# Block two of a two-block transformer kernel: the order of the projection groups, the gates, and who does four small pieces of work

## The chip, the cores and the metric

The kernel runs on one core of a Trainium2 chip. The metric is the device time of one execution in microseconds (us); of several runs of one kernel the median counts. The profiled execution is a run of its own, and the trace divides its time among the engines: TensorE (PE, with its weight loads as PEld), VectorE (DVE), ScalarE (ACT), GpSimd (POOL) and SyncE (SP), which issues the DMAs.

## The reference, cut to what matters

The program is two transformer blocks of two layers each over 256 positions of width 1024, all in float32. The change touches only block two. One of its layers:

```python
h = rmsnorm(x, g_mix)
(qa, ka, va, qb, kb, vb, fl, qc, kc, vc, qi, ki, wi, gl) = split(h @ w_in)
br_a = stick_breaking_attention(qa, ka, va)          # w = exp(log_beta + later sums of log(1 - beta))
br_b = forgetting_attention(qb, kb, vb, cumsum(log_sigmoid(fl + b_forget)))
br_c = indexed_sparse_attention(rope(qc), rope(kc), vc, rope(qi), rope(ki), wi, top_k=64)
gates = sigmoid(gl)                                  # three gates of width 1024
y = gates[0] * (br_a @ w_branch[0]) + gates[1] * (br_b @ w_branch[1]) + gates[2] * (br_c @ w_branch[2])
x = x + y @ w_out
x = x + square(relu(rmsnorm(x, g_mlp) @ w_up)) @ w_down
```

`br_a` has 8 heads of 64, `br_b` 8 heads, `br_c` 8 query heads over 2 key heads; queries and keys are 256 positions, handled as two blocks `tb` of 128.

## The kernel before, in words

**Products.** Each float32 operand is held as two parts, a rounded high part and the rest, and each product is three matmuls (`mm3`, lines 290 to 292). A weight unit is 256 rows by 512 columns; ScalarE rounds it (line 265) and VectorE subtracts to get the rest (line 267; GpSimd does it for a few units of the first group). Units are loaded six ahead and split three ahead, in the order of the list `units`.

**Groups.** A projection of 512 columns is a group of four units. `proj` keeps the activations stationary and gives rows of positions: per unit 12 matmuls of 512 columns. `projT` keeps the weights stationary and gives the transposed result: per unit 24 matmuls of 256 columns. In block two the value groups VA and VB use `proj`, whose evacuation is one ScalarE copy per `tb`; the query and key groups QA, KA, QB, KB use `projT`, whose evacuation is a multiply on VectorE and a split on ScalarE and VectorE. The order is ORDER2: KCQI, QC, the small group TAIL (key of the index, forget logits, index weights), QB, KB, VB, QA, KA, VA, then for each of three merges (branch c, b, a) gate half 0, product half 0, gate half 1, product half 1, then the output projection `w_out` and the MLP.

**Tasks and turns.** The attention work is written as Python generators (tasks) in a queue. `tick()` takes the next two tasks and runs each to its next `yield`, which is a turn. `proj` calls `tick` once per unit and `tb` (8 times a group), `projT` twice per unit and pair of column blocks (16 times a group). So a turn's place is fixed by where the main loop is. The tasks of a layer are `ki_task` and `lf_task` (index key; log of the forget gates, its running sum by TensorE at line 1630), `dsa_task` (index scores, then eight rounds of `max` and `match_replace` per `tb` for the top 64, lines 1666 to 1668, then attention over four pairs of heads), `fox_task` (attention of branch b over four pairs), and `sb_task` (stick-breaking). `join` runs a task to its end, and stands ahead of the first product of its branch. Below that, the Tile framework orders each engine's instructions when the program is built: by place in the program, but an instruction whose operands it estimates to be late lets later ones pass. What comes out is one fixed order per engine; on the chip an engine waits at the head of its list.

**`attend`** (lines 1462 to 1489), for one pair of heads and one `tb`: scores by TensorE; bias and row maximum by VectorE (1471); exponentials and row sums by ScalarE (1476); reciprocal and two multiplies by VectorE (1478, 1480); after one `yield` the transposes by TensorE (1485); their copies by VectorE and ScalarE (1489).

**`sb_task`**: six score tiles of 128x512; Abs and Exp by ScalarE; then per tile Ln by ScalarE (1780), an add by VectorE (1781), a mask by VectorE (1788), another by GpSimd (1790), with a `yield` after every second tile; then per tile a rounded copy and the rest, both by GpSimd (1796, 1798); then the sums over positions as matmuls with a triangle, the high part first (1802) and the rest behind it (1803); Exp; the products with the values (1821, 1822).

**`merge_tok`** (line 1402): gates through tanh on ScalarE (1410), products gated by VectorE (1419) and added up by GpSimd or, for the last branch, by VectorE (1427). The last branch's sums are transposed by small tasks that begin with two empty turns (`Yt.put`), and the output projection follows.

Of the kernel before, what the change touches and what calls it, by code (L numbers as in the profile page):

```python
# [11 lines left out]
F32 = mybir.dt.float32  # L12
# [7 lines left out]
P = 128  # L20
# [18 lines left out]

KCQI, QC, QA, KA, VA, QB, KB, VB, GL = range(9)  # L40
TAIL = -1
ORDER2 = [KCQI, QC, TAIL, QB, KB, VB, QA, KA, VA]
MERGE2 = (2, 1, 0)


# [55 lines left out]
def two_block_kernel(ctx: ExitStack, tc: tile.TileContext, A, out):  # L101
# [28 lines left out]
    def t2(shape, dtype=F32):  # L130

        return T(kp, shape, "k2", dtype)
# [39 lines left out]
    def spawn(gen):  # L172
        t = Task(gen)
        tasks.append(t)
        return t
# [10 lines left out]
    def serial(*gens):  # L186
        for g in gens:
            yield from g
# [38 lines left out]
    for l in range(DEPTH):  # L227
        slowly(1 + l)
        for n in ORDER2:
            if n == TAIL:  # L230
                units += [A["w_tail"][l]]
            else:
                units += [A["w_in_2"][l, n, k] for k in range(4)]
        for b in MERGE2:
            for c in range(2):
                units += [A["w_in_2"][l, GL + 2 * b + c, k] for k in range(4)]
                units += [A["w_bo_2"][l, b, c, k] for k in range(2)]
        for c in range(2):
            units += [A["w_out_2"][l, c, k] for k in range(4)]
        for f in range(9):  # L240
            if f == 0:
                slowly(3)
            if f < 8:
                units += [A["w_up"][l, f, k] for k in range(4)]
            if f:
                units += [A["w_down"][l, c, 2 * (f - 1) + k] for k in range(2) for c in range(2)]
# [637 lines left out]
        for l in range(DEPTH):  # L884
            dve.tensor_scalar(nlam[:, l:l + 1], lam[:, l:l + 1], LAM_INIT[l], -1.0, op0=ALU.add, op1=ALU.mult)

    def neg_log1p_exp(o, x, n, pool_):

        e = T(pool_, [P, n], "lp_e")
        a = T(pool_, [P, n], "lp_a")  # L890
        s = T(pool_, [P, n], "lp_s")
        q = T(pool_, [P, n], "lp_q")
        dve.scalar_tensor_tensor(a, x, -1.0, x, op0=ALU.mult, op1=ALU.max)
        act.activation(e, a, AF.Exp, scale=-1.0)
        dve.tensor_scalar(a, e, 2.0, None, op0=ALU.add)
        dve.reciprocal(a, a)
        dve.tensor_tensor(s, e, a, op=ALU.mult)
        dve.tensor_tensor(q, s, s, op=ALU.mult)
        dve.memset(e, 1.0 / 19)
        for k in range(8, -1, -1):  # L900
            dve.tensor_tensor(e, e, q, op=ALU.mult)
            dve.tensor_scalar(e, e, 1.0 / (2 * k + 1), None, op0=ALU.add)
            yield
        dve.tensor_tensor(e, e, s, op=ALU.mult)
        dve.tensor_scalar(a, x, 0.0, None, op0=ALU.min)
        dve.scalar_tensor_tensor(o, e, -2.0, a, op0=ALU.mult, op1=ALU.add)
# [492 lines left out]
                split(*yT.t[k], y.pop(k), scale=0.5)  # L1399
            projT(2, operands, ev_o, n=n, ticks=1)  # L1400

    def merge_tok(bi, acts, waits, oT, operands, y, yT, rms=None):


        for c in range(2):
            gt = {}

            def ev_gate(tb, ps):
                t = gt[tb] = t2([P, 512])
                act.activation(t, ps, AF.Tanh, scale=rms(tb, True) if rms else 0.5)  # L1410
            if c == 0:
                ts = waits + [spawn(serial(after(waits), g)) for g in oT]
            proj(4, acts, ev_gate)
            if c == 0:
                join(ts)

            def ev_o(tb, ps):
                t = gt.pop(tb)
                dve.scalar_tensor_tensor(t, t, 1.0, ps, op0=ALU.add, op1=ALU.mult)
                if bi == 0:  # L1420
                    y[tb, c] = t
                    return
                ys = y[tb, c]
                if bi == 1:
                    pool.tensor_tensor(ys, ys, t, op=ALU.add)
                    return
                dve.tensor_tensor(ys, ys, t, op=ALU.add)
                yT.put(tb, c, y.pop((tb, c)), 2)
            proj(2, {tb: operands(tb) for tb in acts}, ev_o)

    def by_block(br):

# [9 lines left out]
    xb = [xb[0], xb[1]]  # L1442


    SHE, SLE = pool, pool
    tri = cp.tile([P, 2, P], F32R, name="tri")
    dve.tensor_copy(tri[:, 0], C("negge"))
    dve.tensor_copy(tri[:, 1], C("negone"))
# [13 lines left out]
    def attend(tb, pair, scores, bias, v, pT):  # L1462

        S_ = P * (tb + 1)
        ps = sm_bank()[:, :2 * S_].rearrange("p (j s) -> p j s", j=2)
        scores(ps, tb, pair, S_)
        yield
        z = t2([P, 2, 256])[:, :, :S_]
        st = small(8)
        for j in range(2):  # L1470
            dve.tensor_tensor_reduce(z[:, j], ps[:, j], bias(tb, 2 * pair + j), 1.0, -3.0e38,
                                     op0=ALU.add, op1=ALU.max, accum_out=st[:, j:j + 1])
        dve.tensor_scalar(st[:, 2:4], st[:, 0:2], -1.0, None, op0=ALU.mult)
        yield
        for j in range(2):
            act.activation(z[:, j], z[:, j], AF.Exp, bias=st[:, 2 + j:3 + j], accum_out=st[:, 4 + j:5 + j])
        yield
        dve.reciprocal(st[:, 6:8], st[:, 4:6])
        for j in range(2):
            dve.tensor_scalar(z[:, j], z[:, j], st[:, 6 + j:7 + j], None, op0=ALU.mult)  # L1480
        yield
        pt = sm_bank()[:, :2 * S_].rearrange("p (j s) -> p j s", j=2)
        for j in range(2):
            for sb in range(tb + 1):
                pe.transpose(pt[:, j, sb * P:(sb + 1) * P], z[:, j, sb * P:(sb + 1) * P], ident)  # L1485
        yield
        for j in range(2):
            o = pT[j][:, 0:P] if tb == 0 else pT[j][:, P:3 * P]
            (act.copy if j else dve.tensor_copy)(o, pt[:, j])
# [11 lines left out]
    def block2_layer(l, hT, rms):  # L1501
# [114 lines left out]
        def lf_task():  # L1616
            yield from after([t_ki])

            f2 = lambda t: t.rearrange("p a b -> p (a b)")
            yield from neg_log1p_exp(f2(lf), f2(lfx), 16, tp)  # L1620
            lf2 = T(tp, [P, 2, 40], "lf2")
            pool.memset(lf2, 0.0)
            for k in range(2):
                dve.tensor_copy(lf2[:, :, 32 * k:32 * k + 8], lf)

            nlo = cst[:, COFF["negle"][0]:COFF["negle"][0] + 256]
            for _ in range(LFY):
                yield
            ps = sm_bank()[0:40, 0:256]
            pe.matmul(ps, lf2[:, 0], nlo, start=True, stop=False)  # L1630
            pe.matmul(ps[:, P:], lf2[:, 1], nlo[:, :P], start=False, stop=True)
            yield
            par = C("par")
            for k in range(2):
                act.activation(cs[0:40, k], ps, AF.Copy, scale=par[0:40, k:k + 1])
            for k in range(2):
                dve.scalar_tensor_tensor(cs[32:40, k], ps[32:40], par[32:40, k:k + 1], cs[32:40, k].bitcast(F32),
                                         op0=ALU.mult, op1=ALU.subtract)
# [4 lines left out]
        def dsa_task():  # L1643
            yield from after(t_c + [t_ki])
            for tb in range(2):
# [4 lines left out]
                for p_ in range(2):  # L1650
# [6 lines left out]
                    for j in range(2):  # L1657
# [2 lines left out]
                            dve.tensor_scalar(scv, r[:, j], wv[:, 0:1], None, op0=ALU.mult)  # L1660
                        else:
                            dve.scalar_tensor_tensor(scv, r[:, j], wv[:, i:i + 1], scv, op0=ALU.mult, op1=ALU.add)
                    yield
                dve.tensor_tensor(scv[:, tb * P:], scv[:, tb * P:], causal, op=ALU.add)
                m8 = small(8)
                for it in range(8):
# [4 lines left out]
                dve.tensor_scalar(M, scv, -2.0e38, -NEG, op0=ALU.is_lt, op1=ALU.mult)  # L1671
                dve.tensor_scalar(M, M, NEG, None, op0=ALU.add)
                dve.tensor_tensor(M[:, tb * P:], M[:, tb * P:], causal, op=ALU.add)
                yield

            def scores(ps, tb, pair, S_):
                qh, ql = (t[:, pair % 2, tb * P:(tb + 1) * P] for t in qcT[pair // 2])
# [10 lines left out]
        t_dsa = spawn(dsa_task())  # L1688


        qbT = [(t2([P, 2, 256], F32R), t2([P, 2, 256], F32R)) for _ in range(2)]
        kbdB = [(zeros4(), zeros4()) for _ in range(2)]

# [7 lines left out]
                r = slice(64 * j, 64 * j + 64)  # L1701
                split(*(t[r, :, j] for t in kbdB[q]), ps[r])
        projT(4, hT.mov, ev_kb)
        vb = {}

        def ev_vb(tb, ps):
            vb[tb] = t2([P, 512])
            act.activation(vb[tb], ps, AF.Copy, scale=rms(tb))
        proj(4, acts, ev_vb)

        def fox_task():
            yield from after([t_lf])

# [26 lines left out]
        def ev_ka(q, ps):  # L1740
            split(*kaT[q], scaled(ps))
        projT(4, hT.mov, ev_ka)
        va = {}

        def ev_va(tb, ps):
            va[tb] = t2([P, 512])
            act.activation(va[tb], ps, AF.Copy, scale=rms(tb))
        proj(4, acts, ev_va)

        def sb_task():  # L1750

            zs, ss = [], []
# [25 lines left out]
            dve.tensor_scalar(one, ss[5][:, 0:1], 0.0, 1.0, op0=ALU.mult, op1=ALU.add)  # L1778
            for i in range(6):
                act.activation(ss[i], ss[i], AF.Ln, bias=one)  # L1780
                dve.scalar_tensor_tensor(ss[i], zs[i], 0.0, ss[i], op0=ALU.max, op1=ALU.add)

                def diag(t):
# [9 lines left out]
            sh, sl = {}, {}  # L1793
            for i in (4, 5, 0, 1, 2, 3):
                sh[i] = t2([P, 512], F32R)
                SHE.tensor_copy(sh[i], ss[i])  # L1796
                sl[i] = t2([P, 512], F32R)
                SLE.tensor_tensor(sl[i], ss[i], sh[i].bitcast(F32), op=ALU.subtract)  # L1798
                yield
            for i in (4, 5, 0, 1, 2, 3):  # L1800
                ps = sm_bank()
# [27 lines left out]
        yT = Yt()  # L1829
        waits = {0: [t_sb], 1: [t_fox], 2: [t_dsa]}  # L1830
        for bi, b in enumerate(MERGE2):
            merge_tok(bi, acts, waits[b], [], lambda tb, b=b: by_block(brT[b])(tb), y, yT, rms)
        ya = {tb: yT.stat(tb) for tb in range(2)}
        h2, rms_h = Joined(), Rms()

# [170 lines left out]
```

## Time and profile before

| | us |
|---|---|
| runs of the kernel before | 1831.52, 1832.32, 1834.10 (median 1832.32) |
| the profiled execution | 1833.04 |
| its span, first to last instruction | 1831.2 |
| TensorE busy | 1802.8 (98%) |
| VectorE busy | 1232.3 (67%) |
| ScalarE busy | 907.8 (50%) |
| GpSimd busy | 172.0 (9%) |
| DMA, mean busy share of 16 engines | about 45% |

Block two's first layer runs from about 930 us of the span (its first group) to about 1380, its second from about 1380 to the end; the part that the change touches is the first 250 us of each. The granted clock of TensorE is full in nearly all slices (mean 0.998). A matmul's duration in the trace is that of one in a pipeline, so durations overlap; where nothing is in the way, one of 512 columns starts 0.23 us behind the last and one of 256 columns 0.12 us.

### The profile page before, as it was taken

The page shows a single profiled execution, that of the slowest core. Times are in us where ns is not written, and L with a number is a line of the kernel's source. Part 1 is how long each engine was busy: PE and PEld are TensorE (multiplying, and loading weights), DVE is VectorE, ACT ScalarE, POOL GpSimd, SP SyncE. Part 2 cuts the span into 40 slices and gives each one's busy share as a digit, 9 for nine tenths or more (in the row PEclk, how much of TensorE's full clock was granted, in tenths as well). Part 3 has the DMA queues.
Part 4 walks back from the last instruction along what each step waited for, and adds up shares of the span by engine and source line. Part 5 has one row for each costly group of instructions (what it writes and reads, how often), then busy time and mean ns, then how long its engine had stood idle before and what let it go on. Part 6 is the DMA issues. An engine that isn't in the chain of part 4 may idle for free.

```text
span 1831.2 us, 25010 instructions
## 1 busy us (share of the span) xinstructions
PE 1802.8 (98%) x9256; PEld 1487.8 (81%) x9256; DVE 1232.3 (67%) x2482; ACT 907.8 (50%) x1613; POOL 172.0 (9%) x123
## 2 busy tenths in 40 slices
PE   8999999999999999999999999999999999999998
PEld 4888888887888988888788777888888877788886
DVE  4754546566794935477779887565567978665665
ACT  4623333444343533465464684455566568455553
POOL 2020000001100101001020015000002003300000
PEclk9999999999999999999999999999999999999999
DMA  9533224233471522445744355455554435555552
GB/s 331 176 127 115 97 67 136 93 104 105 146 245 56 169 92 82 143 156 184 264 150 139 121 167 172 151 174 193 185 187 157 139 120 180 171 164 172 184 191 97
DMA packets 83611, 279.30 MB, mean 153 GB/s; under 512 B 13856, under 2 KB 14240, under 8 KB 83360
## 3 DMA queue, kind: packets, MB, share of 16 engines
q1 hardware_dynamic: 83488, 277.70, 45.1%
q8 instruction: 73, 1.20, 0.3%
q14 instruction: 50, 0.41, 0.1%
HBM read 276.61 MB, written 1.05 MB: 152 GB/s over the span
## 4 chain that ended last, share of the span: by engine, by line
PE 41%; DVE 6%; POOL 2%; ACT 2%; issue 1%; DMA 1%; DVEq 0%; POOLq 0%; ACTq 0%
PE mm L290 9%; PE mm L291 9%; PE mm L292 9%; PE sm L436 6%; PE sm L437 3%; DVE k L267 2%; PE sm L497 1%; PE sm L1496 1%; POOL k L1798 1%; PE sm L1485 1%; DVE k L298 1%; POOL k L1796 1%; PE sm L290 1%; DVE k L1668 1%; DMA k<-in_w_modT 1%
## 5 line engine op out<-in xcount | busy, mean ns | idle before, releaser
L290 PE MATMUL mm<-k,k 128*128 128x512 f32 (+1 forms) x2192 | 835.0, 381 | 3.0 <-ACT k L521 2.2
L292 PE MATMUL mm<-k,k 128*128 128x512 f32 (+1 forms) x2192 | 821.6, 375 | 0.3 <-DVE k L523 0.3
L291 PE MATMUL mm<-k,k 128*128 128x512 f32 (+1 forms) x2192 | 821.6, 375 | 0.0
L267 DVE TENSOR_TENSOR k<-k,k 128x1024 fp32r<-128x1024 f32 x449 | 559.8, 1264 | 171.9 <-ACT k L265 113.7
L265 ACT ACTIVATE k<-k 128x1024 fp32r<-128x1024 f32 x458 | 473.2, 1056 | 312.3 <-DVE k L267 134.8
L290 PEld LDWEIGHTS mm<-k,k 128*128 128x128 f32 x2192 | 413.2, 189 | 79.1 <-issue 6.0
L292 PEld LDWEIGHTS mm<-k,k 128*128 128x128 f32 x2192 | 413.1, 188 | 76.4 <-DVE k L523 1.4
L291 PEld LDWEIGHTS mm<-k,k 128*128 128x128 f32 x2192 | 413.6, 189 | 67.1 <-issue 0.5
L436 PE MATMUL sm<-k,k 128*128 128x512 f32 x448 | 158.7, 398 | 0.0
L437 PE MATMUL sm<-k,k 128*128 128x256 f32 x448 | 125.8, 281 | 0.0
L436 PEld LDWEIGHTS sm<-k,k 128*128 128x128 f32 x448 | 84.2, 188 | 20.6
L1872 DVE TENSOR_TENSOR k<-sm,k 128x256 f32<-128x256 f32 x56 | 22.6, 423 | 108.2 <-ACT k L1871 108.2
L1871 ACT ACTIVATE k<-sm 128x256 f32<-128x256 f32 x56 | 21.5, 384 | 130.6 <-PE sm L437 130.6
L707 DVE CUSTOM_DVE_ANT_0 k<-k,k 128x1024 f32<-128x1024 f32 x56 | 68.9, 1234 | 24.4 <-PE mm L291 20.3
L437 PEld LDWEIGHTS sm<-k,k 128*128 128x128 f32 x448 | 84.6, 189 | 0.5
L298 DVE TENSOR_TENSOR k<-sm,k 128x256 fp32r<-128x256 f32 (+2 forms) x78 | 31.9, 414 | 32.5 <-ACT k L297 31.6
L297 ACT ACTIVATE k<-sm 128x256 fp32r<-128x256 f32 (+2 forms) x78 | 28.7, 374 | 45.4 <-PE sm L497 17.5
L968 POOL TENSOR_TENSOR k<-k,k 128x512 f32<-128x512 f32 x16 | 23.4, 1469 | 287.2 <-DVE k L966 286.3
L267 POOL TENSOR_TENSOR k<-k,k 128x1024 fp32r<-128x1024 f32 x9 | 21.3, 2402 | 297.9 <-DVE k L1839 229.4
L483 ACT ACTIVATE k<-k 128x512 f32<-128x512 f32 x36 | 22.6, 628 | 47.7 <-DVE k L1839 20.6
L974 ACT ACTIVATE k<-mm 128x512 f32<-128x512 f32 x30 | 17.8, 596 | 54.1 <-PE mm L292 53.9
L1222 ACT ACTIVATE k<-sm,small 128x512 f32<-128x512 f32 (+1 forms) x48 | 29.1, 614 | 21.1 <-DVE small L1220 20.5
(299 smaller groups left out, 1705.3 us busy)
## 6 DMA issues: line engine op xcount, KB each, us to landing
k<-in_w_in SPq DMA_DIRECT2D x248, 512.0 KB, 3.4
k<-in_w_up SPq DMA_DIRECT2D x64, 512.0 KB, 3.9
k<-in_w_down SPq DMA_DIRECT2D x64, 512.0 KB, 3.8
k<-in_w_bo SPq DMA_DIRECT2D x48, 512.0 KB, 3.5
k<-in_w_modT SPq DMA_DIRECT2D x32, 512.0 KB, 3.4
k<-in_w_out SPq DMA_DIRECT2D x32, 512.0 KB, 3.6
k<-in_w_mod SPq DMA_DIRECT2D x16, 512.0 KB, 7.3
k<-in_c_rows SPq DMA_DIRECT2D x5, 512.0 KB, 3.7
```

Source lines behind the costliest of these rows:

```text
L265: act.activation(h, r, AF.Copy)
L267: (pool if i in slow else eng).tensor_tensor(lo, r, h.bitcast(F32), op=ALU.subtract)
L290: pe.matmul(ps, lh, rh, start=start, stop=False)
L291: pe.matmul(ps, lh, rl, start=False, stop=False)
L292: pe.matmul(ps, ll, rh, start=False, stop=stop)
L297: act.activation(h, src, AF.Copy)
L298: dve.tensor_tensor(lo, src, h.bitcast(F32), op=ALU.subtract)
L436: pe.matmul(ps[q], wh[:, k, s], acts.both(kt), start=(kt == 0), stop=False)
L437: pe.matmul(ps[q][:, :256], wl[:, k, s], acts.high(kt), start=False, stop=(kt == 2 * nk - 1))
L707: dve.tensor_tensor_reduce(o, w, sb[s], 0.5, 0.0, op0=ALU.mult, op1=ALU.add, accum_out=res[:, s, i - 1:i])
L968: pool.tensor_tensor(o, o, tt, op=ALU.add)
L1222: act.activation(e, ps[m], AF.Exp, scale=0.125, bias=st[:, 2 + m:3 + m], accum_out=st[:, 4 + m:5 + m])
```

## The change

ORDER2 becomes KCQI, QC, TAIL, VB, VA, QB, KB, QA, KA, and the two value groups move up in the code; `fox_task` is now spawned after KB and `sb_task` after KA. In block two's merges both gate halves come ahead of the `join` and both product halves behind it, with the list of units in the same order. In `attend` the second head's multiply moves to ScalarE, and two `yield`s instead of one stand ahead of the transposes. The 18 small operations (9 rounds of multiply and add, on 128x16 elements) of the series for the forget gates move to GpSimd, run without a `yield` between them, and six `yield`s follow. In `dsa_task` one `yield` per block goes after the index scores, and one ahead of the second block's scores. In `sb_task` the six Ln stand together ahead of the loop over the rest, and the rounded copy moves to ScalarE. In block one `merge_tok` keeps its order.

```diff
-ORDER2 = [KCQI, QC, TAIL, QB, KB, VB, QA, KA, VA]
+ORDER2 = [KCQI, QC, TAIL, VB, VA, QB, KB, QA, KA]
...
                 units += [A["w_in_2"][l, GL + 2 * b + c, k] for k in range(4)]
+            for c in range(2):
                 units += [A["w_bo_2"][l, b, c, k] for k in range(2)]
...
-    def neg_log1p_exp(o, x, n, pool_):
+    def neg_log1p_exp(o, x, n, pool_, eng=dve):
...
         for k in range(8, -1, -1):
-            dve.tensor_tensor(e, e, q, op=ALU.mult)
-            dve.tensor_scalar(e, e, 1.0 / (2 * k + 1), None, op0=ALU.add)
-            yield
+            eng.tensor_tensor(e, e, q, op=ALU.mult)
+            eng.tensor_scalar(e, e, 1.0 / (2 * k + 1), None, op0=ALU.add)
+            if eng is dve:
+                yield
+        if eng is not dve:
+            yield from wait(6)
...
+        ts = waits + [spawn(serial(after(waits), g)) for g in oT]
+        gates(0)
+        if both:
+            gates(1)
+        join(ts)
+        products(0)
+        if not both:
+            gates(1)
+        products(1)
...
         dve.reciprocal(st[:, 6:8], st[:, 4:6])
-        for j in range(2):
-            dve.tensor_scalar(z[:, j], z[:, j], st[:, 6 + j:7 + j], None, op0=ALU.mult)
-        yield
+        dve.tensor_scalar(z[:, 0], z[:, 0], st[:, 6:7], None, op0=ALU.mult)
+        act.activation(z[:, 1], z[:, 1], AF.Copy, scale=st[:, 7:8])
+        yield from wait(2)
...
-            yield from neg_log1p_exp(f2(lf), f2(lfx), 16, tp)
+            yield from neg_log1p_exp(f2(lf), f2(lfx), 16, tp, pool)
...
-                    yield
+                    if p_ == 0:
+                        yield
...
-                yield
+                if tb:
+                    yield
...
             for i in range(6):
                 act.activation(ss[i], ss[i], AF.Ln, bias=one)
+            for i in range(6):
                 dve.scalar_tensor_tensor(ss[i], zs[i], 0.0, ss[i], op0=ALU.max, op1=ALU.add)
...
-                SHE.tensor_copy(sh[i], ss[i])
+                act.activation(sh[i], ss[i], AF.Copy)
                 sl[i] = t2([P, 512], F32R)
-                SLE.tensor_tensor(sl[i], ss[i], sh[i].bitcast(F32), op=ALU.subtract)
+                pool.tensor_tensor(sl[i], ss[i], sh[i].bitcast(F32), op=ALU.subtract)
...
-            merge_tok(bi, acts, waits[b], [], lambda tb, b=b: by_block(brT[b])(tb), y, yT, rms)
+            merge_tok(bi, acts, waits[b], [], lambda tb, b=b: by_block(brT[b])(tb), y, yT, rms, True)
```

## Rows read from the trace of the kernel before

**Rows 1.** The page: busy us (share of the span) and instructions of each engine
```profile
PE 1802.8 (98%) x9256; PEld 1487.8 (81%) x9256; DVE 1232.3 (67%) x2482; ACT 907.8 (50%) x1613; POOL 172.0 (9%) x123
```
**Rows 2.** Waits of TensorE from 800 us on: us in total, times, longest
```profile
PE sm L1803 <- POOL k L1798: 2.6, 4, 1.0
PE sm L1485 <- DVE k L1480: 2.2, 2, 1.1
...
PE sm L1630 <- DVE lf L1624: 0.8, 1, 0.8
PE sm L1630 <- issue: 0.7, 1, 0.7
PE sm L1608 <- DVE lp_a L895: 0.5, 2, 0.2
```
**Rows 3.** Timeline of TensorE at the triangle sums: start, us, instruction, idle before it
```profile
1101.53 0.39 PE L292 MATMUL mm<-k,k 128*128 128x512 f32 x1
1101.75 0.39 PE L1802 MATMUL sm<-k,tri 128*128 128x512 f32 x1
1103.11 0.50 PE L1803 MATMUL sm<-k,tri 128*128 128x512 f32 x1 [0.96 <-POOL k L1798]
...
1106.19 0.39 PE L1802 MATMUL sm<-k,tri 128*128 128x512 f32 x1
```
**Rows 4.** Timeline of GpSimd in the same stretch
```profile
1097.21 2.08 POOL L1790 TENSOR_TENSOR k<-k,cst 128x512 f32<-128x512 f32 x1
1099.23 1.61 POOL L1796 CAST k<-k 128x512 fp32r<-128x512 f32 x1
1100.92 2.13 POOL L1798 TENSOR_TENSOR k<-k,k 128x512 fp32r<-128x512 f32 x1
```
**Rows 5.** Timeline of ScalarE at the six Ln
```profile
1083.31 1.28 ACT L1780 ACT_TABLE_LOAD   x1
1084.61 2.57 ACT L1780 ACTIVATE k<-k,small 128x512 f32<-128x512 f32 x4
1087.19 1.28 ACT L1410 ACT_TABLE_LOAD   x1
1088.48 1.26 ACT L1410 ACTIVATE k<-mm,rms 128x512 f32<-128x512 f32 x2
1089.77 1.28 ACT L1780 ACT_TABLE_LOAD   x1
1091.06 1.34 ACT L1780 ACTIVATE k<-k,small 128x512 f32<-128x512 f32 x2
```
**Rows 6.** Stretches of layer one: us, busy us (instructions) of each engine, clock, DMA share
```profile
962.00:985.00 23.00, 22.25 (x158) 20.61 (x159) 22.12 (x76) 10.97 (x17) 1.33 (x2) 1.00 0.48 161
985.00:1005.00 20.00, 18.88 (x130) 17.30 (x129) 19.32 (x55) 9.16 (x15) 2.43 (x3) 1.00 0.39 132
1005.00:1060.00 55.00, 54.95 (x316) 43.03 (x317) 43.04 (x140) 34.85 (x92) 0.00 (x0) 1.00 0.36 116
1060.00:1098.00 38.00, 38.00 (x184) 30.42 (x183) 32.51 (x57) 34.18 (x53) 8.06 (x8) 1.00 0.55 180
```
**Rows 7.** Groups of VectorE by line and shape, 955 to 1010 us: busy, mean ns
```profile
L267 DVE TENSOR_TENSOR k<-k,k 128x1024 fp32r<-128x1024 f32 x14 | 17.1, 1220 | 1.4 <-ACT k L265 0.9 <-ACT k L1476 0.5
L1667 DVE MAX8 small<-k 128x8 f32<-128x256 f32 x8 | 3.4, 426 | 0.2
L1668 DVE MATCH_REPLACE8 k<-small,k 128x256 f32<-128x256 f32 x8 | 3.3, 410 | 0.0
...
L901 DVE TENSOR_TENSOR lp_e<-lp_e,lp_q 128x16 f32<-128x16 f32 x9 | 1.6, 172 | 0.1
L902 DVE TENSOR_SCALAR lp_e<-lp_e 128x16 f32<-128x16 f32 x9 | 1.5, 169 | 0.2
...
L1480 DVE TENSOR_SCALAR k<-k,small 128x128 f32<-128x128 f32 x4 | 1.0, 284 | 0.0
```
**Rows 8.** Timeline of ScalarE around 1003 us
```profile
1002.06 1.25 ACT L1708 ACTIVATE k<-mm,rms 128x512 f32<-128x512 f32 x2
1003.20 0.40 ACT L1476 ACTIVATE k<-k,small 128x128 f32<-128x128 f32 x1
```
**Rows 9.** Groups of GpSimd by line and shape, whole span: busy, mean ns
```profile
L1790 POOL TENSOR_TENSOR k<-k,cst 128x256 f32<-128x256 f32 x8 | 7.0, 892 | 199.0 <-DVE k L1781 199.0
...
L1622 POOL MEMSET lf<- 128x80 f32 x2 | 0.3, 164 | 0.3 <-POOLq L1998 0.3
```
**Rows 10.** Timeline of VectorE at the end of the last merge
```profile
1168.39 0.69 DVE L1419 SCALAR_TENSOR_TENSOR k<-k,mm 128x512 f32<-128x512 f32 x1 [4.92 <-PE mm L292]
1169.19 0.69 DVE L1427 TENSOR_TENSOR k<-k,k 128x512 f32<-128x512 f32 x1
...
1172.17 0.69 DVE L301 SCALAR_TENSOR_TENSOR k<-sm,k 128x512 fp32r<-128x512 f32 x1 [0.90 <-ACT k L300]
```
**Rows 11.** Timeline of TensorE there
```profile
1173.04 0.48 PE L290 MATMUL mm<-k,k 128*128 128x512 f32 x1
```

More of the change, by code (lines that the diff above doesn't have):

```diff
@@ L1400, in merge, with merge_tok, gates, ev @@
             projT(2, operands, ev_o, n=n, ticks=1)
[L1402 to L1409, printed above, removed]
-                act.activation(t, ps, AF.Tanh, scale=rms(tb, True) if rms else 0.5)
[L1411 to L1418, printed above, removed]
+    def merge_tok(bi, acts, waits, oT, operands, y, yT, rms=None, both=False):
+        gt = {}
+        def gates(c):
+            def ev(tb, ps):
+                t = gt[tb, c] = t2([P, 512])
+                act.activation(t, ps, AF.Tanh, scale=rms(tb, True) if rms else 0.5)
+            proj(4, acts, ev)
+        def products(c):
+            def ev(tb, ps):
+                t = gt.pop((tb, c))
                 dve.scalar_tensor_tensor(t, t, 1.0, ps, op0=ALU.add, op1=ALU.mult)
@@ L1428, in ev_o @@
                 yT.put(tb, c, y.pop((tb, c)), 2)
-            proj(2, {tb: operands(tb) for tb in acts}, ev_o)
+            proj(2, {tb: operands(tb) for tb in acts}, ev)
+        ts = waits + [spawn(serial(after(waits), g)) for g in oT]
[7 more added lines that the diff above has]
+        products(1)
     def by_block(br):
@@ L1442, in two_block_kernel @@
     xb = [xb[0], xb[1]]
-    SHE, SLE = pool, pool
     tri = cp.tile([P, 2, P], F32R, name="tri")
@@ L1688, in block2_layer, with ev_vb, ev_va @@
         t_dsa = spawn(dsa_task())
+        vb = {}
+        def ev_vb(tb, ps):
+            vb[tb] = t2([P, 512])
+            act.activation(vb[tb], ps, AF.Copy, scale=rms(tb))
+        proj(4, acts, ev_vb)
+        va = {}
+        def ev_va(tb, ps):
+            va[tb] = t2([P, 512])
+            act.activation(va[tb], ps, AF.Copy, scale=rms(tb))
+        proj(4, acts, ev_va)
         qbT = [(t2([P, 2, 256], F32R), t2([P, 2, 256], F32R)) for _ in range(2)]
@@ L1703, in block2_layer @@
         projT(4, hT.mov, ev_kb)
[L1704 to L1709, printed above, removed]
         def fox_task():
@@ L1742, in block2_layer @@
         projT(4, hT.mov, ev_ka)
[L1743 to L1748, printed above, removed]
         def sb_task():
```

## The prediction

> **What bounds the kernel now.** I read the page's busy times first: TensorE is busy 98% of the span, and the next engine, VectorE, 67% [rows 1]. The change neither adds nor removes a matmul, so all it can win is time in which TensorE stands still, and all it can lose is new standing still. Therefore the second view is the waits of TensorE itself in the part where block two runs. They are few: the low part of the triangle sums waits for GpSimd (2.6 us in four waits), the transposes of a division wait for VectorE (2.2 us in two), the running sum of the forget gates 1.5 us in two, the index key 0.5 us [rows 2]. Both layers show the same, so half of each is one layer's.
>
> What a wait costs is a little more than its idle time. At the triangle the matmul of line 1803 starts 1.36 us behind that of 1802, where 0.22 us is usual (1101.53 to 1101.75): lost 1.13 us, though the row calls 0.96 us idle [rows 3]. I add 0.17 us per wait: 3.3 us for the triangle, 2.5 us for the divisions, 1.8 us for the running sum, 0.8 us for the index key. 8.4 us, or 0.46% of the time, is all that there is to win.
>
> **The triangle sums.** GpSimd does two operations per tile, the cast (1.61 us) and the subtraction (2.13 us), 3.74 us together [rows 4]. TensorE comes to the next tile after 4.44 us (1101.75 to 1106.19), of which 1.13 us were the wait, so after 3.3 us when nothing stops it [rows 3]: GpSimd is the slower one, and TensorE waits for it until the lead has been regained. With the cast on ScalarE GpSimd needs 2.13 us a tile and stays ahead. ScalarE pays six copies of 128x512, about 0.62 us each by a scaled copy of that shape [rows 8], 3.7 us a layer. It gets back two table loads: the trace has Ln x4, a load, two tanh of a gate, a load, Ln x2, and six Ln in a row need neither of the two loads in the middle, 2 x 1.28 = 2.6 us [rows 5]. What is late next is the mask on GpSimd ahead of the subtractions (2.08 us for the last tile, beside VectorE's work), one operation ahead of six of 2.13 us. I take the whole 3.3 us; the bounds are 0 and 3.3 us.
>
> The Trainium skill ("ScalarE: Activation LUTs", section "What ACT_TABLE_LOAD costs") puts a switch of tables at about 2.66 us, the load and a drain of 1.38 us behind it. Here the first Ln starts 1.30 us after the load's start (1083.31 to 1084.61), so no row shows the drain [rows 5], and the measurement decides. By the page ScalarE would gain 5.3 us a layer instead of 2.6 us; the sum would be the same, since the triangle's wait has gone either way.
>
> **The first division.** Between the small group and the first attention VectorE is full: 22.12 of 23 us, then 19.32 of 20 us [rows 6]. The transposes wait at the end of this stretch. In it lie the 18 small operations of the forget gates (3.1 us), the top-64 rounds (0.43 + 0.41 us each for a block of 256, plus a load of values) and the weight units' subtractions at 1.22 us [rows 7], and the evacuations of QB and KB. The change takes off the 3.1 us, and half of each division: 0.28 us on VectorE for about 0.40 us on ScalarE by an Exp of that shape [rows 7, 8], 16 times a layer. It also puts VB and VA, which VectorE doesn't evacuate, into the first 22 us. Against it: those groups give 8 + 8 turns where QB and KB gave 16 + 16, so counted by turns the index scores come two units before VA's end instead of near QB's end, some 8 us later, and the top-64 of the second block then falls into QB and KB, with 0.7 us between turns and some 0.9 us of VectorE per round beside the units. By turns the first transposes come in KB instead of at QA's start, while VectorE's backlog is not smaller. The build's order moves such an instruction back by its own estimate; how well can't be read here. Bounds: the whole 2.5 us won, or as much lost. I take half, 1.2 us, since VectorE has less to do in all. The extra turn hides the division where VectorE isn't behind; it lengthens the attention of a branch by 8 turns, which end ahead of the joins: counted through, task c ends with the last turn of its gates and the others earlier, as before.
>
> **The forget gates' series on GpSimd.** No row shows such a small operation there. From below: a fill of 128x80 takes 0.164 us; from above: an addition of 128x256 takes 0.89 us [rows 9]. Eighteen in a chain are 3.0 to 16 us. I take 0.2 us, near the fill, since 16 columns are nearer to 80 than to 256: 3.6 us. The time there is: by turns the task starts at VA's second unit and reaches line 1630 in QB's second, about 4 turns of 1.36 us and 4 half units of 1.44 us, 11 us; off that go the operations before and behind the series on VectorE and ScalarE, eight or so at 0.17 us with their hand-overs, some 2.4 us. So 8.6 us are free, 0.48 us an operation. At 0.2 us the running sum would come in time, but its last operations still queue on the full VectorE: of the 1.8 us I take 0.6 us. Bounds: 1.8 us won, and 16 - 8.6 = 7.4 us a layer lost. The index key's 0.8 us stay.
>
> **Gates and products.** Both gate halves ahead of the join give task c 8 more turns. The price is at the last merge: both product halves stand together, and only the output projection is behind them. Per half VectorE does, for each `tb`, 0.69 + 0.69 us and later a split of 0.69 us [rows 10]. Already the half that is used last is split at 1172.86 and used at 1173.04 [rows 10, 11]: 0.18 us of slack. In the new order VectorE has, between the end of the first half and that of the second, 2.8 us of sums, 1.4 us of splits and up to two units at 1.22 us, 6.6 us, in 5.4 us of TensorE's time. It can be 1.2 us late. Then the other `tb`, whose operands are ready, can fill. Bounds 0 and 2 us for both layers; I take 0.4 us.
>
> Two groups' units and the gates' units are loaded in the new order, by as many DMAs on SP's queue and as far ahead as before; TensorE has no wait for a DMA there [rows 2], and I cost it at nothing. The remaining edits (fewer turns ahead of the index scores, the places of the spawns, ScalarE's 16 divisions of 0.4 to 0.5 us) I cost at nothing. What hides them is that TensorE always has a projection at hand; ScalarE is busy 34.85 of 55 us and then 34.18 of 38 us [rows 6], and 4 us more in the second stretch would delay tanh and rounded units, which are three units ahead. If that cover went, it would be some 1 us a layer; rather nothing below.
>
> **The sum.** 3.3 + 1.2 + 0.6 - 0.4 = 4.7 us won. The profiled execution took 1833.04 us, its span 1831.2 us and 1.8 us around it; less 4.7 us, 1828.3 us. That execution lay 0.7 us above the median of the runs (1832.32), so I predict 1827.6 us.
>
> **Rivals.**
>
> *Everything goes.* All of the four waits vanish and the end of the merge costs nothing: 8.2 us, 1824.1 us. For it: the change touches each of these chains. Against it: VectorE stays full between the small group and the attention, since four `projT` groups, which it evacuates, now follow one another.
>
> *The waits only move.* The triangle's 3.3 us go, but the first division, now in KB, waits as long as before or longer, and the merge's end takes 2 us: about 1 us won, 1831.3 us. For it: full VectorE [rows 6] and 0.18 us of slack [rows 10, 11]. Against it: 3.1 us less in the full stretch, and the other `tb` as filler.
>
> *GpSimd's chain is too slow.* It decides from 0.48 us an operation. At 0.7 us the chain takes 12.6 us, is 4 us late in each layer, and TensorE stands at line 1630 with the index scores and the projection queued behind: 8 us lost, and with 3.3 + 1.2 - 0.4 us won the time is 1836.2 us. For it: the row at 0.89 us, and that each operation needs the last one's result. Against it: the fill at 0.164 us, and that 16 columns are a sixteenth of 256 [rows 9]. The Trainium skill ("GPSIMD Engine Reference", section 4.1) counts elementwise work of two inputs about twice as long on GpSimd as on VectorE; by that an operation would take an estimated 0.34 us, the chain 6.1 us, and nothing would wait. No run so far shows it.
>
> **How the numbers follow.** The forecast has 0.47, everything goes 0.08, the waits only move 0.28, GpSimd too slow (with what else might make it late) 0.17. The forecast's own range is 1826 to 1830 us. The range goes from 1823.5 us (below which not even the whole 8.4 us leads) to 1836.5 us (just past the slow chain at 0.7 us; its top, 7.4 us a layer, is left out). About 0.2%, 3.7 us, is what a measurement of this kernel can tell from no change: below 1828.7 us is faster, above 1836.0 us slower. Of the forecast's 0.47 some 0.38 lie below 1828.7 us; with 0.08 and a part of the moving waits that makes 0.51 faster. Of the last case 0.14 lie above 1836 us. 0.35 remain.
>
> **What would show it.** Right: no wait of line 1803 for GpSimd, two table loads of Ln fewer in each layer, a shorter wait at 1485, TensorE's busy time as before and its idle time 4 to 5 us less. Wrong: a wait of several us at line 1630 for GpSimd or what follows it, with the 18 operations above 0.48 us each; waits of the output projection's transposes or matmuls on line 1427 or the split; or waits of a unit's rounding behind ScalarE's divisions.

## The result: 0.5% slower

The changed kernel takes 1842.35 us (median of five runs, 1840.85 to 1843.40) against 1832.32 us. The ratio is 1.0052 [1.0041, 1.0063]. The prediction was 1827.6 us with a range up to 1836.5 us: wrong in sign and outside the range. The profiled execution took 1842.62 us, 9.6 us more than that of before, with a span of 1840.8 us.

### The profile after

The page of the changed kernel, busy us of each engine, to be read beside [rows 1]:

```profile
PE 1806.8 (98%) x9255; PEld 1492.0 (81%) x9256; DVE 1219.9 (66%) x2414; ACT 920.5 (50%) x1653; POOL 159.9 (9%) x147
```

VectorE has 12.4 us less to do, ScalarE 12.7 us more, and the time went up all the same: the share of busy time decides nothing here. TensorE's waits in the changed kernel do (us in total, times, longest); line 1496 is the transposes of a division, 1485 in [rows 2], and 1490 its multiply on VectorE:

```profile
PE sm L1496 <- DVE k L1490: 13.1, 4, 4.1
```

Of the waits in [rows 2], those of the triangle, the running sum and the index key are gone. What was 2.2 us in two waits at the division has become 13.1 us in four. In TensorE's timeline of layer one (start, us, instruction, idle before it) the four are two places, the first division of the index branch and the last of branch b:

```profile
1005.10 0.33 PE L1496 MATMUL sm<-cst,k 128*128 128x128 f32 x1 [2.53 <-DVE k L1490]
...
1101.33 1.09 PE L1496 MATMUL sm<-cst,k 128*128 128x128 f32 x4 [4.08 <-DVE k L1490]
1102.07 0.78 PE L293 MATMUL mm<-k,k 128*128 128x512 f32 x1
1102.64 0.63 PE L291 MATMUL mm<-k,k 128*128 128x512 f32 x1
1103.07 0.63 PE L292 MATMUL mm<-k,k 128*128 128x512 f32 x1
1103.49 0.63 PE L293 MATMUL mm<-k,k 128*128 128x512 f32 x1
```

Behind the second wait, matmuls of 512 columns start 0.43 us apart, not the usual 0.23. The windows show why (us; busy us and instructions of PE, PEld, DVE, ACT, POOL; granted clock; DMA share; GB/s). The granted clock is 0.50 behind both waits, 1.2 GHz in place of 2.4:

```profile
1002.60:1005.10 2.50, 0.00 (x0) 0.00 (x0) 2.41 (x11) 1.29 (x5) 0.00 (x0) 1.00 0.37 147
1005.40:1008.80 3.40, 3.40 (x16) 3.10 (x14) 1.68 (x8) 0.91 (x4) 0.00 (x0) 0.50 0.02 5
1008.80:1012.00 3.20, 3.20 (x28) 3.20 (x28) 3.17 (x6) 3.15 (x8) 0.00 (x0) 1.00 0.48 166
1097.30:1100.90 3.60, 0.00 (x0) 0.00 (x0) 3.60 (x4) 3.00 (x5) 3.51 (x2) 1.00 0.00 0
1101.00:1104.30 3.30, 2.97 (x9) 2.57 (x10) 3.30 (x4) 0.54 (x2) 1.31 (x2) 0.50 0.42 153
...
1459.40:1462.70 3.30, 2.88 (x11) 2.60 (x12) 0.99 (x6) 1.61 (x3) 0.00 (x0) 0.50 0.00 0
1555.00:1561.70 6.70, 5.79 (x20) 3.99 (x21) 5.89 (x5) 2.54 (x5) 4.08 (x4) 0.50 0.48 157
```

The account over both layers: the four waits cost 13.8 us (start to start, less the usual distance), and the matmuls at half clock another 1.44 + 1.48 + 1.40 + 2.52 = 6.8 us. The lost waits of before were 8.4 us. 13.8 + 6.8 - 8.4 = 12.2 us; TensorE's time through block two grew by 9.6 us. The other 2.6 us were won in distances between matmuls too short to stand as a wait, which I did not divide further.

### Why the first division is later

VectorE in the changed kernel, layer one, at the forget gates (908 is the multiply behind the series, 1635 the copies for the running sum):

```profile
966.43 0.28 DVE L299 TENSOR_TENSOR k<-sm,k 64x128 fp32r<-64x128 f32 x1 [1.79 <-ACT k L298]
967.05 0.29 DVE L299 TENSOR_TENSOR k<-sm,k 64x128 fp32r<-64x128 f32 x1 [0.34 <-ACT k L298]
972.16 0.18 DVE L908 TENSOR_TENSOR lp_e<-lp_e,lp_s 128x16 f32<-128x16 f32 x1 [4.82 <-POOL lp_e L903]
972.37 0.18 DVE L910 SCALAR_TENSOR_TENSOR lf<-lp_e,lp_a 128x16 f32<-128x16 f32 x1
972.58 0.25 DVE L1635 COPY lf<-lf 128x16 f32<-128x16 f32 x2
972.75 1.22 DVE L268 TENSOR_TENSOR k<-k,k 128x1024 fp32r<-128x1024 f32 x1
```

and GpSimd meanwhile (1536 is a fill of another task's tiles):

```profile
962.67 2.86 POOL L1536 MEMSET k<- 128x1024 f32 x3 [31.49 <-DVE k L268]
965.50 0.22 POOL L902 TENSOR_TENSOR lp_e<-lp_e,lp_q 128x16 f32<-128x16 f32 x1
965.81 0.27 POOL L903 TENSOR_SCALAR lp_e<-lp_e 128x16 f32<-128x16 f32 x1
966.16 0.22 POOL L902 TENSOR_TENSOR lp_e<-lp_e,lp_q 128x16 f32<-128x16 f32 x1
...
967.61 0.95 POOL L1536 MEMSET k<- 128x1024 f32 x1
...
971.88 0.25 POOL L903 TENSOR_SCALAR lp_e<-lp_e 128x16 f32<-128x16 f32 x1
```

The series is one pair every 0.65 us, 0.33 us an operation, and takes 6.6 us with a fill of 0.95 us that stands between its operations. Three more fills stand ahead of it, so that it begins at 965.50, 1 us after VectorE had its operands ready (964.45). The pace is below the 0.48 us from which it was to hurt. But its reader, line 908, stands at the head of VectorE's list right behind the last work before the series, and everything else waits behind it: VectorE is idle for 4.8 us at the start of the very stretch that was full before [rows 6].

### Why branch b's last division is late

VectorE and then GpSimd ahead of the second wait. Lines 1795, 1802, 1804 and 1812 are the add, the two masks and the subtraction of stick-breaking; 268 is a weight unit's; 1489 and 1490 are the division:

```profile
1093.41 1.28 DVE L1795 SCALAR_TENSOR_TENSOR k<-k,k 128x512 f32<-128x512 f32 x2
1094.61 3.08 DVE L1802 TENSOR_TENSOR k<-k,cst 128x512 f32<-128x512 f32 x2
1097.62 0.15 DVE L1489 RECIPROCAL small<-small 128x2 f32<-128x2 f32 x1
1097.69 2.21 DVE L268 TENSOR_TENSOR k<-k,k 128x1024 fp32r<-128x1024 f32 x1
1099.83 1.35 DVE L1490 TENSOR_SCALAR k<-k,small 128x256 f32<-128x256 f32 x1
```

```profile
1094.23 2.92 POOL L1804 TENSOR_TENSOR k<-k,cst 128x512 f32<-128x512 f32 x2 [2.31 <-DVE k L1795]
1097.11 5.20 POOL L1812 TENSOR_TENSOR k<-k,k 128x512 fp32r<-128x512 f32 x3
```

Counted in turns, branch b's last transposes came one gate unit ahead of the Ln before; now they come three turns behind stick-breaking's first tiles, so the division queues among its masks. The traces agree: before, its last multiply on VectorE starts at 1069.31 us and the Ln at 1084.61 [rows 5]; now the Ln start at 1085.37 and the multiply at 1099.83. GpSimd is busy throughout, and beside it VectorE's operations are long: 1.35 us for a multiply that takes 0.34 us elsewhere (below, first experiment), 2.21 us for a subtraction of 1.22 us. That GpSimd is so busy there because the six Ln now stand together, and the masks of all tiles come at once, is my reading of the order; no run takes it by itself.

### The profile page after: what moved, and what is told of

It is laid out like the page before. It is cut to its first block, busy times and chain, and to the rows that moved or that the text cites. A ratio compares the mean times of both kernels' runs of the same rounds, so it can differ in the third digit from the quotient of the medians.

```text
span 1840.8 us, 24973 instructions
## 1 busy us (share of the span) xinstructions
PE 1806.8 (98%) x9255; PEld 1492.0 (81%) x9256; DVE 1219.9 (66%) x2414; ACT 920.5 (50%) x1653; POOL 159.9 (9%) x147
## 5 line engine op out<-in xcount | busy, mean ns | idle before, releaser
L268 DVE TENSOR_TENSOR k<-k,k 128x1024 fp32r<-128x1024 f32 x449 | 553.5, 1251 | 184.4 <-ACT k L266 115.9
```

The source lines that it names most:

```text
L268: (pool if i in slow else eng).tensor_tensor(lo, r, h.bitcast(F32), op=ALU.subtract)
```

## The experiments

Each ratio is to the kernel before on the same chip, with its 95% interval. The first nine ask about the two waits, the last three about the parts that win.

**One turn ahead of the transposes**, as before; the rest as changed.

```diff
-        yield from wait(2)
+        yield
```

> The changed kernel with one turn instead of two ahead of the transposes in attend. Theory (collision): the long wait of TensorE for the division (4.1 us a layer) is branch b's last attention, which by the count of turns now falls three turns behind the start of the stick-breaking splits, among that task's VectorE and GpSimd work; with one turn it comes ahead of the Ln, so that wait goes, with the half-clock stretch behind it, and the short one (2.5 us a layer) stays: 1830 to 1834 us. Rival (order): the wait belongs to the new order of the groups, and one turn changes it little: 1839 to 1843 us. Rival (load): VectorE is simply too full there with the cast and the six Ln moved, and the wait comes back on another instruction: 1838 to 1843 us.

1841.16 us, 1.0040 [1.0028, 1.0053]: a miss. TensorE's waits in it:

```profile
PE sm L1496 <- DVE k L1490: 5.0, 2, 2.5
PE sm L1817 <- POOL k L1812: 2.9, 2, 1.4
```

Branch b's wait is gone, which ties it to the turns, and the first division's is not. But the triangle (1817) waits again, half clock is behind the first wait in both layers, and the time hardly falls. The rest went into short distances: taken from one matmul's start to the next, less the usual distance and half clock aside, those of at most 0.5 us sum to some 30 us in block two, against 23 us in the changed kernel (the last experiment but one comes back to them). Here the multiply runs ahead of the masks, on VectorE with GpSimd idle:

```profile
1087.81 0.34 DVE L1490 TENSOR_SCALAR k<-k,small 128x256 f32<-128x256 f32 x1
```

**The old order of groups**; the rest as changed.

```diff
-ORDER2 = [KCQI, QC, TAIL, VB, VA, QB, KB, QA, KA]
+ORDER2 = [KCQI, QC, TAIL, QB, KB, VB, QA, KA, VA]
```

(and the two value groups moved back in the code)

> The changed kernel with the old order of the groups (QB, KB, VB, QA, KA, VA), all else as changed. Theory (collision): by turns branch b's last transposes come ahead of the Ln again although the extra turn stays, and the top 64 no longer falls into QB and KB, so both waits go, while the triangle's and the running sum's waits stay away: 1825 to 1829 us, faster than both kernels. Rival (turn): the extra turn is what costs, and the long wait stays: 1836 to 1842 us. Rival (gates): the two gate halves ahead of the products cost at the last merge: 1832 or more, with waits of the output projection.

1837.19 us, 1.0024 [1.0015, 1.0033]: a miss. Branch b's wait is gone, so it takes both the order and the turns to make it; its last multiply (1088.87 us) is ahead of the Ln (1092.81 us) again. The first division's grew:

```profile
PE sm L1496 <- DVE k L1490: 9.1, 2, 4.5
```

So the order was not the reason for the first wait, as I had supposed.

**The Exp and Ln wait for branch b's attention**; the rest as changed. The new line stands ahead of the Exp, and so of the Ln behind them:

```diff
+            yield from after([t_fox])
             for i in range(6):
                 act.activation(ss[i], ss[i], AF.Exp, scale=-1.0)
```

> The changed kernel, but the stick-breaking task waits with its Exp and Ln, and so with all that GpSimd does for it, until branch b's task is done; order, turns and gates as changed. Theory (collision): nothing but the overlap of the two tasks makes the long wait, so it goes (4.1 us a layer and the half clock behind it), the short wait stays, and the later stick-breaking work still ends ahead of its join: 1830 to 1835 us. Rival (order or turn by themselves): no change, 1840 to 1843 us.

1830.60 us, 0.9989 [0.9980, 0.9998]: as expected. One line takes 1.0052 to 0.9989, some 11.5 us, more than the whole loss. The long wait is gone and no triangle wait is back; only the first division's remains, with half clock behind it in the second layer alone:

```profile
PE sm L1496 <- DVE k L1490: 5.0, 2, 2.5
```

**The kernel before with the six Ln together, the copy on ScalarE, and the series on GpSimd.**

```diff
-            yield from neg_log1p_exp(f2(lf), f2(lfx), 16, tp)
+            yield from neg_log1p_exp(f2(lf), f2(lfx), 16, tp, pool)
...
+            for i in range(6):
                 act.activation(ss[i], ss[i], AF.Ln, bias=one)
...
-                SHE.tensor_copy(sh[i], ss[i])
+                act.activation(sh[i], ss[i], AF.Copy)
```

(and the function of the series as in the change)

> The kernel before with only the cast on ScalarE, the six Ln together, and the series of the forget gates on GpSimd. Theory: the triangle's waits (3.3 us lost) and the running sum's (1.8 us) go and nothing comes: 1827 to 1829 us. Rival: VectorE's full stretch ahead of the first division only hands the time on, and the first division waits longer: 1829 to 1832 us.

1839.25 us, 1.0033 [1.0022, 1.0044]: a miss, and the run that showed the reason. With order, gates and attention all as before, the first division (here 1488) waits far longer than in [rows 2], and VectorE (second fence) stands behind the series just as in the changed kernel:

```profile
PE sm L1488 <- DVE k L1483: 7.9, 2, 4.0
```

```profile
964.71 0.29 DVE L298 TENSOR_TENSOR k<-sm,k 64x128 fp32r<-64x128 f32 x1
969.10 0.18 DVE L907 TENSOR_TENSOR lp_e<-lp_e,lp_s 128x16 f32<-128x16 f32 x1 [4.10 <-POOL lp_e L902]
```

**The same without the series on GpSimd** (the first edit of the diff undone).

> The kernel before with only the cast on ScalarE and the six Ln together, the series left on VectorE. Theory (blocked queue): this is b_sums_lp without the blocked queue, so the first wait is 1.1 us as before, the triangle's wait is gone: 1828 to 1830 us. Rival (these two edits made the loss of b_sums_lp): 1835 to 1839 us again.

1828.63 us, 0.9979 [0.9970, 0.9988]: as expected. 3.8 us below the kernel before, where the term was 3.3 us; the triangle's wait is gone and the others are as in [rows 2]. Between this kernel and the one ahead of it the series alone costs some 10 us (0.9979 against 1.0033).

**The changed kernel with the series back on VectorE.**

```diff
-            yield from neg_log1p_exp(f2(lf), f2(lfx), 16, tp, pool)
+            yield from neg_log1p_exp(f2(lf), f2(lfx), 16, tp)
```

> The changed kernel with the series of the forget gates back on VectorE, with its yields. Theory (blocked queue): with the series on GpSimd, VectorE's next operation on it stands at the head of VectorE's queue and VectorE idles 4.1 to 4.8 us a layer; all its work up to the first division comes that much later, and TensorE waits there. With the series back on VectorE that idle time is gone, the first wait falls from 2.5 us to 1.2 us or less, and the long wait for branch b's last division (4.1 us) stays: 1834 to 1838 us. Rival (full VectorE, the new order's top-64 in QB and KB): VectorE has 3 us more work in the same stretch and the first wait grows to 3 us or more: 1842 to 1846 us.

1838.74 us, 1.0035 [1.0022, 1.0047]: 0.7 us above what was expected. The first wait falls from 2.5 to 1.75 us in each layer, not to 1.2 us, and no half clock follows it; the long one stays:

```profile
PE sm L1496 <- DVE k L1490: 11.6, 4, 4.1
```

The first wait falls so little because the series takes VectorE 5.8 us there (964.71 to 970.48 us), with two of its adds, of 0.86 and 1.02 us, beside GpSimd's fills: line 908 comes at 970.51 us, only 1.65 us earlier than in the changed kernel. The intervals of this kernel and of the changed one overlap, so the 3 us between them are not secured by these two alone.

**The same with the Ln waiting for branch b** (both edits above).

> The changed kernel with the series on VectorE and the Ln of the stick-breaking task behind branch b's task. Both causes are taken away: by the two theories together neither wait is left above 1.2 us, and no stretch at half clock in block two: 1822 to 1827 us, below both kernels. If the first wait comes from the new order itself, 1830 us or more, as with the Ln alone.

1827.22 us, 0.9972 [0.9961, 0.9984]: 0.2 us above what was expected. There is no half clock in block two, and one pair of waits is left, above the 1.2 us that were expected:

```profile
PE sm L1496 <- DVE k L1490: 3.5, 2, 1.8
```

The two causes together are more than the whole loss: 1842.35 becomes 1827.22 us.

**Sixteen empty turns behind the series in place of six**, with the Ln waiting for branch b.

```diff
-            yield from wait(6)
+            yield from wait(16)
```

> The changed kernel with the Ln behind branch b's task, the series on GpSimd as changed, but 16 empty turns behind it instead of 6. Theory (blocked queue): it is the place of VectorE's next operation on the series, not GpSimd's slowness, that costs; ten turns later VectorE has other work ahead of it and idles less than 1 us there, so the first wait falls to 1.2 us or less: 1822 to 1828 us. Rival (slow GpSimd, or the series' result late by itself): VectorE's idle time stays or TensorE now waits at the running sum: 1829 to 1834 us.

1832.24 us, 0.9997 [0.9988, 1.0006]: a miss, and within the rival's range. VectorE still stands at line 908:

```profile
DVE lp_e L908 <- POOL lp_e L903: 4.8, 1, 4.8
```

Where the reader stands on VectorE's list is not decided by its turn; ten turns later in the program it is at the same place. That leaves the build's ordering by its own estimates; what it estimates for the series I have not measured. Between the theory and the rival the next run decides.

**Everything behind the series on GpSimd too**, with the Ln waiting for branch b.

```diff
-        dve.tensor_tensor(e, e, s, op=ALU.mult)
+        eng.tensor_tensor(e, e, s, op=ALU.mult)
...
+            eng.tensor_scalar(e, e, -2.0, None, op0=ALU.mult)
+            eng.tensor_tensor(o, e, a, op=ALU.add)
...
-                dve.tensor_copy(lf2[:, :, 32 * k:32 * k + 8], lf)
+                pool.tensor_copy(lf2[:, :, 32 * k:32 * k + 8], lf)
```

> The changed kernel with the Ln behind branch b's task, and with everything behind the series (the last multiply, the sum, the two copies) on GpSimd too, so that VectorE has no operation that waits for GpSimd there. Theory (blocked queue, by the order that the build writes down): the 4.8 us of VectorE's idle time go, so the first wait falls below the 1.8 us that it has with the series on VectorE, since VectorE has 3 us less to do: 1823 to 1827 us, unless TensorE now waits for GpSimd at the running sum (up to 4 us a layer: 1830 us or more, the rival).

1826.34 us, 0.9965 [0.9953, 0.9978]: as expected, and the lowest time of all. The series is still on GpSimd at the same pace, but nothing on VectorE reads it, and VectorE goes on, after 2.4 us in which it waits for ScalarE:

```profile
966.38 0.29 DVE L299 TENSOR_TENSOR k<-sm,k 64x128 fp32r<-64x128 f32 x1 [0.34 <-ACT k L298]
969.07 1.23 DVE L268 TENSOR_TENSOR k<-k,k 128x1024 fp32r<-128x1024 f32 x1 [2.40 <-ACT k L266]
```

```profile
PE sm L1500 <- DVE k L1494: 3.3, 2, 1.6
```

It was the wait on VectorE's list, not GpSimd's pace: against the kernel with the Ln waiting and the reader on VectorE (0.9989 [0.9980, 0.9998]) the intervals are just apart. The gain over the kernel with the series on VectorE (0.9972) is within the intervals.

**Three kernels on the parts that win**, all with the series on VectorE. The first two have the Ln waiting for branch b as well, and are read against 1827.22 us; the third has not, and is read against 1838.74 us.

Gates and products in the old order:

```diff
-            merge_tok(bi, acts, waits[b], [], lambda tb, b=b: by_block(brT[b])(tb), y, yT, rms, True)
+            merge_tok(bi, acts, waits[b], [], lambda tb, b=b: by_block(brT[b])(tb), y, yT, rms)
```

(and the list of units in the same order)

> The best kernel so far (changed kernel, series on VectorE, Ln behind branch b: 1827.2 us) with block two's merges in the old order: one gate half, one product half, and again. If both halves' gates are worth what they were meant for, the join now finds branch c unfinished by some turns and TensorE waits ahead of a product: 1829 to 1835 us. If they are worth nothing: 1826 to 1829 us.

1831.32 us, 0.9988 [0.9980, 0.9997]: 4.1 us more in the medians, but the intervals (0.9961 to 0.9984 for the other) overlap, and no wait ahead of a product came. TensorE's idle waits are the same 3.5 us in two. In the profiled executions TensorE's work of block two is 2.5 us longer here, and 1.5 us of that is a stretch at half clock behind the first division (from 1006.29 us), where no gate has been reached. So in these two executions about 1 us is left that the gates' order can be worth; a gain is not secured.

One turn ahead of the transposes (the diff of the first experiment):

> The same best kernel with one turn instead of two ahead of the transposes. If the extra turn hides the divisions, waits at the transposes appear: 1828 to 1832 us. If the build's order hides them anyway: 1826 to 1828 us.

1833.90 us, 1.0010 [1.0001, 1.0019]: the second turn is worth some 7 us here, more than either side expected, and hardly as waits (3.8 us in three). The products with the values (1507 and 1508; TensorE's busy us and mean ns, layer one) show it. First with one turn, then with two:

```profile
L1507 PE MATMUL sm<-k,k 128*64 128x256 f32 x32 | 9.3, 404 | 0.0
L1508 PE MATMUL sm<-k,k 128*64 128x128 f32 x32 | 5.6, 273 | 0.0
```

```profile
L1507 PE MATMUL sm<-k,k 128*64 128x256 f32 x32 | 6.9, 403 | 0.0
L1508 PE MATMUL sm<-k,k 128*64 128x128 f32 x32 | 4.3, 273 | 0.0
```

The same 64 matmuls, of the same mean length, cover 14.9 and 11.2 us, since they overlap less. Not all of that is lost. By the distance from start to start less the usual one, these two lines lose 10.2 us over both layers with one turn and 5.1 us with two: 5.1 us of the 7, in pieces too small to stand as a wait. The kernel before, with one turn and the whole division on VectorE, loses 5.2 us there (its matmuls cover 11.9 us), so the second turn mostly pays for what the other edits made later.

```profile
L1496 PE MATMUL sm<-k,k 128*64 128x256 f32 x32 | 7.3, 404 | 0.0
L1497 PE MATMUL sm<-k,k 128*64 128x128 f32 x32 | 4.6, 273 | 0.0
```

The old order of groups, the Ln not waiting:

> The changed kernel with the series back on VectorE and the old order of the groups; gates, turns, ScalarE's division and the stick-breaking edits as changed, no wait of the Ln. Theory: order and series are the whole loss. By turns branch b's last transposes come ahead of the Ln, VectorE isn't blocked, so neither wait is above 1.3 us and no stretch runs at half clock: 1825 to 1829 us. Rival (gates, turns or ScalarE's division lose too): 1830 us or more.

1829.39 us, 0.9983 [0.9974, 0.9991]: 0.4 us above what was expected, with a first wait of 1.9 us, not 1.3, and half clock behind it in the second layer. Without the new order and the series on GpSimd, the changed kernel is faster than before. The running sum (1641) waits again:

```profile
PE sm L1496 <- DVE k L1490: 3.7, 2, 1.9
...
PE sm L1641 <- DVE lf L1635: 0.6, 1, 0.6
PE sm L1641 <- issue: 0.6, 1, 0.6
```

It did not wait with the series on VectorE in the new order, nor with the series on GpSimd in the old one: either edit takes that wait away. Beside the kernel with the old order and the series on GpSimd (1.0024) this is the series' price once more, some 7.5 us, with intervals apart.

## Why the prediction was wrong, point by point

- *The triangle sums, 3.3 us won.* Right. The wait is gone, and done alone it measured 3.8 us (0.9979, 2.2 to 5.5 us by its interval). ScalarE has six Ln in a row behind one table load, as the working had it:

```profile
1084.07 1.28 ACT L1793 ACT_TABLE_LOAD   x1
1085.37 3.79 ACT L1793 ACTIVATE k<-k,small 128x512 f32<-128x512 f32 x6
```

- *The forget gates' series, 0.6 us won.* The step that failed first. I took 0.2 us an operation and set 0.48 us as the point from which it hurts; it was 0.33 us, on the safe side, and yet it hurt. I counted nothing for GpSimd's own fills either, which took some 2 us ahead of the series and in it. The 8.6 us that I called free were counted by turns to line 1630, TensorE's read. The first reader is VectorE, and I didn't say who queues behind that reader: all of VectorE's work, for 4.8 us. The rival had the right chain and the wrong place. The running sum lost its wait; the loss came out 33 us later, at the first division. The Trainium skill ("GPSIMD Engine Reference", section 4.1) counts elementwise work of two inputs about twice as long on GpSimd as on VectorE, from which I had estimated 0.34 us an operation, twice VectorE's busy time of 0.17 us. That the pace came out at 0.33 us is luck: in the same chain VectorE too needs 0.21 us from start to start (967.08, 967.29, 967.50 us with the series back on it), and the busy times are 0.22 and 0.25 us, so GpSimd took 1.3 to 1.6 times as long here. That nothing would wait was my conclusion, and it was wrong.
- *The first division, 1.2 us won.* Wrong in sign; in the changed kernel it idles 2.8 us more over both layers (2.5 against 1.1 us a layer), just past the 2.5 us that bounded the loss. Even with the series on VectorE it waits 1.75 us a layer against 1.1 us before, in the new order and (1.9 us) in the old. What makes that is open.
- *The extra turn, "which end ahead of the joins ... as before", nothing.* The step with the largest price. Ahead of the join was true, and not the question: among which work on VectorE branch b's last division falls was. Together with the order it cost 4.1 us idle a layer and, with half clock, some 11.5 us in all, by the run that only makes the Exp and Ln wait. That VectorE's slowing beside GpSimd is the larger part of it is argued from the rows (3.08 + 2.21 + 1.35 = 6.6 us, at undisturbed durations of 0.68, 1.22 and 0.34 us 2.9 us), not tested by itself.
- *0.17 us on top of a wait.* Too low for long ones. In the changed kernel each of four waits of 2.5 to 4.1 us was followed by half clock, at a cost of 1.4 to 2.5 us. The waits of about 1 us in [rows 2], on which the figure rests, had none behind them.
- *Gates and products, 0.4 us lost.* No wait came at the last merge. Without the new order the kernel was no faster; whether the new one gains is not secured.
- The sum without the two causes, 1827.22 us, lies at the predicted 1827.6 us, but by luck and not by its terms. By TensorE's starts, less the usual distances, the triangle gave back 3.6 us, the running sum 1.6 us where 0.6 was taken, and the index key the 0.8 us that were to stay; the transposes of the divisions gave nothing (7.5 us over the usual distances before, 7.9 us now) where 1.2 us were taken.
- A slip that changes nothing: the rival in which everything goes takes 8.2 us where its four waits make 8.4 us.

## What to carry to other kernels

Work moved to an idle engine must have its reader looked at too: an engine that reads the result waits at the head of its list, and everything behind it pays, even if the chain is fast enough for the final use. Ask too what the idle engine has to do just then. When turns are added or groups change places, ask for each small operation on a busy engine what will stand ahead of it there, not only whether it ends in time by the program's order. And price a wait of TensorE with the half clock that may follow it, as those of 2.5 us and more did here.

## What the runs showed of the hardware

- Half clock followed standing still. Of the 16 waits of 2.5 to 4.5 us in block two in the profiled executions above, 15 were followed by a granted 0.50, mostly for 3.4 us, some for 6.8 us, costing 1.4 to 3.3 us; of the 12 waits of 1.6 to 1.9 us two were. It is no sharp line: with the Ln waiting for branch b, two equal waits of 2.5 us had it behind one only.
- VectorE and GpSimd slow each other. Beside GpSimd's masks and subtractions, VectorE's multiply took 1.35 us in place of 0.34, its mask of 128x512 1.54 us where an undisturbed operation of that shape takes 0.68, its subtraction of 128x1024 2.21 us in place of 1.22. GpSimd's subtraction of 128x512 took 1.73 us each beside them (5.20 us for three), and 1.28 us at 1104.74 us, where VectorE was idle for most of the time. The Trainium skill ("GPSIMD Engine Reference", section 8) says that the two share their interfaces to SBUF, and that VectorE's instructions with two inputs there, or in a two-port mode, contend. The trace agrees for the mask and the subtraction, which have two inputs; the multiply has one, and no run shows its mode.
- A dependent operation of 128x16 on GpSimd shows 0.22 us (multiply) and 0.25 us (add) of busy time, and a pair every 0.65 us, against 0.17 us each on VectorE [rows 7].
